# Linear attention: the column sums as dense passes in high and low part, and the values' planes in their result tile

## The chip, the cores and the metric

One core of a Trainium2 chip runs the whole layer. The metric is device microseconds of one execution, median over runs. TensorE (PE) multiplies, VectorE (DVE) and ScalarE (ACT) work elementwise, GpSimd (POOL) does a few elementwise steps, and nearly every transfer is issued from SyncE's queue (SP).

## The reference, cut to what matters

```python
u = rmsnorm(x, g_pre) @ W_in                     # q, k, v, gates of both head groups
log_a = log_sigmoid(g_lr @ w_a2 + b_a) / 16
# gated linear attention, 4 heads, dk = 128, dv = 256, with b = cumsum(log_a):
# scores[i, j] = sum_d q[i, d] k[j, d] exp(b[i, d] - b[j, d])   for j <= i
# out = scores @ v + (q exp(b)) @ state
# stick-breaking attention, 8 heads; then the output product, a norm,
# and a gated embedding product
```

1024 tokens, model width 2048, float32. The change touches only the scores of the linear attention, and the way its values get turned.

## The kernel before, in words

Every operand of a large product is split into a high part (`fp32r`, by a ScalarE copy) and a low part (what is left, by a VectorE subtraction); a product is the three matmuls high x high, low x high, high x low (`split`, L113; `dense`, L158). A "step" is one k-tile of a dense product for both halves of the tokens: six matmuls of 128x512.

The program writes the instructions of the small stages in between by generators. `dense` calls `step()` (L188) after each k-tile, and `step()` advances first the `urgent` generators (the turning of values) and then, at RATE_GLA = 1.0 step for step, the job in turn: `gla(h, ...)`, one linear-attention head at a time, while the projection of the next head's keys, queries and two value tiles runs on TensorE. The numbers W0, W1, W2 and W4 (L48) say how many steps the generator lets pass between its parts. The instructions of an engine are then put in order by a planner that goes by priority (the order of writing) and by what is ready; it can draw an instruction ahead whose inputs and buffer are there. Buffers are tagged (`BUFS`, L303): "E" and "X" have two, "u" twelve, "s" two, "o", "o2", "q" and "kt" one each.

A head is done in two halves of 512 tokens (four chunks of 128; of the second pair of chunks the order is reversed). Per half `gla` does:

1. The gate: one matmul, logarithms, cumulative sums b by four scans (L417 to L425). q exp(b) is made on GpSimd (L439), and the keys for the state in an "E" buffer (L437), which are then split in 16-bit planes by ScalarE and turned by a transposing transfer (`turn_by_dma`, L356).
2. The scores, chunk by chunk, by levels 64, 32, 16, 8, 4, 2, 1: for a level, `factors` (L443) makes k exp(..) and q exp(..) in an "X" buffer, `level` (L461) multiplies them by four matmuls of 128x128 into a "z" bank of PSUM, and `put` (L455) copies by a mask what belongs to the level into the scores `sc`. After level 8 the states are made.
3. Two parts of the scores are no matmul products but sums over the 128 partitions: the diagonal (sum of k*q, `prep_diag`, `put_diag`, L479 to L485) and level 1 (neighbours, `prep_one`, `put_one`, L488 to L500). They are made by `by_rows` (L468): ones with 32 columns against a float32 tile, in four tiles of the array, each giving 32 rows; then four masked copies of 32 partitions each. The diagonal's sums stand directly ahead of level 64, level 1's directly behind level 2.
4. The output of the half in "o" and "o2", its norm (whose mean is a column sum by two dense passes of ones against a high and a low part, `column_sums`, L198), and its store (L571).

Values get turned by `turn` (L364) after their projection: ScalarE splits the tile into planes of 16 bits in an "X" buffer, a transfer transposes them into an "E" buffer, and VectorE copies them together into the result tile (L369).

Of the kernel before, what the change touches and what calls it, by code (L numbers as in the profile page):

```python
# [12 lines left out]
F32R = mybir.dt.float32r  # L13
U8 = mybir.dt.uint8
U16 = mybir.dt.uint16
QT = 256
AF = mybir.ActivationFunctionType
ALU = mybir.AluOpType

P = 128  # L20
D = 2048
T = 1024
HT = 512
# [8 lines left out]
LEVELS = (64, 32, 16, 8, 4, 2, 1)  # L32
# [12 lines left out]


RATE_GLA = 1.0
W0, W1, W2, W4 = 2, 6, (2, 3, 3, 3, 2, 3), 2  # L48
RATE_SB = 0.9
W3 = 4  # L50
V_MID, V_END, VW = ("X", "X"), ("E", "E"), 3
L1, L2, PERIOD = 8, 8, 5
W = 2 * HT
KP = KT // 2
# [8 lines left out]
def layer(ctx, tc, xT, w_in, w_gate, w_lr, w_a2, b_a, g_pre, g_head, w_out, g_post,  # L63
          w_g, b_g, w_p, pT, ident, masks, sel_in, out):
    nc = tc.nc
    V, A, G, PE = nc.vector, nc.scalar, nc.gpsimd, nc.tensor
# [34 lines left out]
    def mm(o, lhsT, rhs, start, stop):  # L101
        PE.matmul(o, lhsT, rhs, start=start, stop=stop)  # L102

    def f(t):
        return t.bitcast(F32)
# [5 lines left out]
    ones_r = const.tile([P, P], F32R, name="ones_r")  # L111

    def split(hi, lo, src, eng=None):  # L113
        A.activation(hi, src, AF.Copy)  # L114
        (eng or V).tensor_tensor(lo, src, f(hi), op=ALU.subtract)  # L115
# [109 lines left out]
    pair = {}  # L225
# [76 lines left out]
    with tc.tile_pool(name="att", bufs=1, reuse_waits="tile") as ap:  # L302
# [11 lines left out]
        def at(tag, shape=(P, HT), dt=F32):  # L314
            pool, bufs = (ap, BUFS[tag]) if tag in BUFS else (own[1], {**GLA_BUFS, **SB_BUFS}[tag])
            return pool.tile(list(shape), dt, tag=tag, name=nm(tag), bufs=bufs)
# [37 lines left out]
            return go  # L354

        def turn_by_dma(src, n, mid, tag):  # L356
            pl = at(mid, (P, 2 * n), U16)
            A.activation(pl.rearrange("p (two n) -> p two n", two=2),  # L358
                         src.bitcast(U16)[:, :2 * n].rearrange("p (n two) -> p two n", two=2), AF.Copy)
            tt = at(tag, (P, 2 * n), U16)  # L360
            nc.sync.dma_start(tt.rearrange("p (c t) -> p c t", t=P), pl, transpose=True)
            return tt.rearrange("p (two c t) -> p two c t", two=2, t=P)

        def turn(vt, dst, parts):  # L364
            w = turn_by_dma(vt, HT, V_MID[parts - 1], V_END[parts - 1])
            for _ in range(VW):
                yield 1
            full = dst if parts == 1 else at("o")
            V.tensor_copy(full.bitcast(U16).rearrange("p (c t two) -> p two c t", c=4, two=2), w)  # L369
            if parts == 2:  # L370
                split(*dst, full)
            yield 1

        def view(t, start, *dims):
            return bass.AP(t.tensor, t.offset + start, [t.ap[0]] + [list(d) for d in dims])
# [28 lines left out]
        def gla(h, kp, qp, vp):  # L404
# [6 lines left out]
            for hf in HALVES:  # L411
# [25 lines left out]
                V.tensor_tensor(ke, ke, k, op=ALU.mult)  # L437
                turned_keys = turn_by_dma(ke, HT, "s", "E")
                G.tensor_tensor(qe, qe, q, op=ALU.mult)  # L439
                for _ in range(W0):  # L440
                    yield 1

                def factors(hl):  # L443
                    ref = view(b, hl - 1, (QT + 1, 2), (2 * hl, P // hl), (0, hl))
                    x = at("X")
                    xk = view(x, 0, (hl, 2), (2 * hl, P // hl), (1, hl))
                    xq = x[:, QT:].rearrange("p (s n h) -> p s n h", s=2, h=hl)
                    V.tensor_tensor(xk, ref, keys(b, hl), op=ALU.subtract)
                    V.tensor_tensor(xq, queries(b, hl), ref, op=ALU.subtract)
                    A.activation(x, x, AF.Exp, scale=1.0 / TAU)  # L450
                    times(xk, xk, keys(k, hl))
                    times(xq, xq, queries(q, hl))
                    return x

                def put(li, z):  # L455
                    hl = LEVELS[li]
                    m = mask_s[:, QT * li:QT * (li + 1)]
                    V.copy_predicated(queries(sc, hl), *(t.rearrange("p (s n h) -> p s n h", s=2, h=hl)
                                                         for t in (m, z[:, :QT])))
# [5 lines left out]
                        mm(to[:, :, j], ch(x, j), moving[:, :, j], True, True)  # L465
                    put(li, z)

                def by_rows(e, n, m):  # L468
                    z = ps("z")
                    rows = [slice(32 * g, 32 * g + 32) for g in range(4)]  # L470
                    for g, r in enumerate(rows):
                        PE.matmul(z[r, :4 * n].rearrange("p (c t) -> p c t", c=4), f(ones_r)[:, :32],
                                  view(e, n * g, (m, 4), (1, n)), start=True, stop=True,
                                  tile_position=(0, 32 * g))
                    return [(r, z[r, :4 * n]) for r in rows]

                def prep_diag():
                    e = at("E")
                    V.tensor_tensor(e, k, q, op=ALU.mult)  # L479
                    return e  # L480

                def put_diag(e):
                    for g, (r, z) in enumerate(by_rows(e, 32, P)):
                        m = mask_s[r, 7 * QT + 32 * g:7 * QT + 32 * g + 32].rearrange("p (c t) -> p c t", c=1)
                        V.copy_predicated(view(sc[r], 32 * g, (P, 4), (1, 32)), m.to_broadcast([32, 4, 32]),  # L485
                                          z.rearrange("p (c t) -> p c t", c=4))

                def prep_one():  # L488
                    e = at("E", (P, QT))
                    e4 = e.rearrange("p (s n h) -> p s n h", s=2, h=1)  # L490
                    V.tensor_tensor(e4, queries(b, 1), keys(b, 1), op=ALU.subtract)
                    A.activation(e, e, AF.Exp, scale=1.0 / TAU)
                    times(e4, e4, keys(k, 1))
                    times(e4, e4, queries(q, 1))
                    return e

                def put_one(e):
                    for g, (r, z) in enumerate(by_rows(e, 16, 64)):
                        with tc.high_priority(offset=800):
                            V.copy_predicated(view(sc[r], 32 * g + 1, (QT - 1, 2), (P, 2), (2, 16)),  # L500
                                              view(mask_s[r], 6 * QT + 16 * g, (P, 2), (64, 2), (1, 16)),
                                              z.rearrange("p (s c t) -> p s c t", s=2, c=2))

                def join_keys():
                    ket = at("kt")
# [14 lines left out]
                            V.scalar_tensor_tensor(S, Ss[-1], eb[:, c:c + 1], d, op0=ALU.mult, op1=ALU.add)  # L520
                        Ss.append(S)

                diag, xs = prep_diag(), factors(LEVELS[0])
                for _ in range(W1):
                    yield 1
                for i in range(6):
                    x, xs = xs, factors(LEVELS[i + 1]) if i < 5 else prep_one()
                    for _ in range(W2[i]):
                        yield 1
                    if i == 0:  # L530
                        ket = join_keys()
                        put_diag(diag)
                    level(i, x)
                    if i == 3:
                        states((0, 1))
# [918 lines left out]
```

## Time and profile before

| what | us |
|---|---|
| median of 3 runs | 2054.58 |
| lowest and highest | 2049.41, 2055.2 |
| profiled execution, its own time | 2058.89 |
| span of the profiled execution | 2057.2 |
| linear attention's stage | about 117 to 545 in the span |

The mean granted TensorE clock is 0.999 of full speed. In the tables of groups each row is a line of the kernel, an engine, an operation, its output and inputs by tile name, the shape and the count, then total busy us, mean ns of one, and the idle time of the engine ahead of it with what ended it. In a timeline each row has the start and the duration in us; a row with x4 stands for four instructions, and a note in brackets is idle time ahead of it with its releaser. Matmuls are pipelined, so the durations of neighbours overlap. L102 is the helper that issues all matmuls but the tiled ones (L472 here, L287 at the start); "dn" is a bank of a dense product, "z" a bank for the small stages.

### The profile page before, as it was taken

How to read it: one execution, taken by the hardware profiler on the slowest of the kernel's cores; microseconds unless marked ns; L12 is line 12 of the kernel's file. 1: busy time of each engine (PE TensorE's matmuls, PEld its weight loads, DVE VectorE, ACT ScalarE, POOL GpSimd, SP SyncE). 2: the span in 40 equal slices, each digit the busy share in tenths (PEclk: the TensorE clock that was granted, in tenths of full speed). 3: DMA queues.
4: the chain of work that ended last, by engine and by line, in shares of the span. 5: the costliest groups of instructions: out<-in, count | busy, mean ns of one | idle time of the engine just before them, and what ended most of it. 6: DMA issues, size and time to landing. Idle time of an engine off the chain costs nothing.

```text
span 2057.2 us, 26551 instructions
## 1 busy us (share of the span) xinstructions
PE 2041.2 (99%) x9632; PEld 1691.3 (82%) x9632; DVE 1466.2 (71%) x2305; ACT 865.9 (42%) x1367; POOL 92.5 (4%) x214
## 2 busy tenths in 40 slices
PE   9999999999999999999999999999999999999998
PEld 7788888888888788888888788888788888878887
DVE  8567777776666676666567677788778778886765
ACT  8333433333455455545457323344233434323332
POOL 0000000000101111101101000000000000000000
PEclk9999999999999999999999999999999999999999
DMA  7122333232244444434335798888888586876762
GB/s 236 53 79 83 89 82 94 82 88 82 86 105 108 96 111 109 115 93 93 79 98 158 262 330 287 310 292 300 315 289 282 167 307 224 301 272 218 235 202 92
DMA packets 237715, 354.90 MB, mean 173 GB/s; under 512 B 132736, under 2 KB 138000, under 8 KB 237584
## 3 DMA queue, kind: packets, MB, share of 16 engines
q1 hardware_dynamic: 236832, 350.97, 53.8%
q10 hardware_dynamic: 720, 2.23, 0.3%
q8 instruction: 75, 1.23, 0.3%
q14 instruction: 56, 0.46, 0.1%
q0 software_dynamic: 32, 0.01, 0.0%
HBM read 249.85 MB, written 73.92 MB: 157 GB/s over the span
## 4 chain that ended last, share of the span: by engine, by line
PE 77%; DVE 10%; DMA 8%; issue 3%; ACT 2%; POOL 0%; SPq 0%; DVEq 0%; POOLq 0%; ACTq 0%
PE dn L102 67%; PE z L102 4%; PE t L102 3%; PE o L102 2%; DVE wl L115 2%; DMA wr<-w_out 1%; DMA ar<-og_d 1%; DVE wr L936 1%; DMA E<-X 1%; DMA wr<-w_g 1%; DMA ar<-h_d 1%; DVE al L115 1%; DMA h_d<-st 1%; DVE ar L933 1%; DVE st L933 0%
## 5 line engine op out<-in xcount | busy, mean ns | idle before, releaser
L102 PE MATMUL dn<-ah,hi 128*128 128x512 f32 x1408 | 558.5, 397 | 1.0 <-ACT ah L271 1.0
L102 PE MATMUL dn<-ah,lo 128*128 128x512 f32 x1408 | 549.4, 390 | 0.0
L102 PE MATMUL dn<-al,hi 128*128 128x512 f32 x1408 | 548.8, 390 | 0.0
L102 PE MATMUL dn<-ah,wl 128*128 128x512 f32 x1216 | 474.4, 390 | 4.0 <-DVE wl L115 3.8
L102 PE MATMUL dn<-ah,wh 128*128 128x512 f32 x1216 | 473.4, 389 | 1.0 <-ACT wh L114 1.0
L102 PE MATMUL dn<-al,wh 128*128 128x512 f32 x1216 | 473.1, 389 | 0.0
L102 PEld LDWEIGHTS dn<-al,hi 128*128 128x128 f32 x1408 | 264.3, 188 | 56.7 <-DVE al L272 0.3
L102 PEld LDWEIGHTS dn<-ah,hi 128*128 128x128 f32 x1408 | 265.0, 188 | 55.0 <-ACT ah L271 3.1
L102 PEld LDWEIGHTS dn<-ah,lo 128*128 128x128 f32 x1408 | 265.1, 188 | 48.5
L114 ACT ACTIVATE wh<-wr 128x1024 fp32r<-128x1024 f32 x152 | 159.7, 1057 | 295.9 <-PE dn L102 221.2
L102 PEld LDWEIGHTS dn<-ah,wl 128*128 128x128 f32 x1216 | 228.3, 188 | 55.1 <-DVE wl L115 7.8
L102 PEld LDWEIGHTS dn<-ah,wh 128*128 128x128 f32 x1216 | 228.3, 188 | 48.8 <-ACT wh L114 2.0
L102 PEld LDWEIGHTS dn<-al,wh 128*128 128x128 f32 x1216 | 228.3, 188 | 47.3
L115 DVE TENSOR_TENSOR wl<-wr,wh 128x1024 fp32r<-128x1024 f32 x152 | 185.1, 1219 | 10.5 <-ACT wh L114 10.3
L114 ACT ACTIVATE hi<-raw 128x512 fp32r<-128x512 f32 x192 | 120.1, 626 | 149.4 <-PE dn L102 146.1
L115 DVE TENSOR_TENSOR lo<-raw,hi 128x512 fp32r<-128x512 f32 x192 | 131.4, 685 | 53.4 <-ACT hi L114 53.1
L358 ACT ACTIVATE X<-E 128x256 uint16<-128x256 uint16 (+2 forms) x96 | 81.1, 844 | 130.7 <-DVE E L640 65.5
L635 DVE TENSOR_TENSOR_SCAN X<-X 128x128 f32<-128x128 f32 (+2 forms) x96 | 98.0, 1021 | 15.7 <-POOL X L629 14.2
L650 DVE COPY v<-E 128x512 uint16<-128x512 uint16 (+1 forms) x160 | 64.3, 429 | 47.3 <-DMA E<-X 44.1
L115 DVE TENSOR_TENSOR s<-v,s 128x512 fp32r<-128x512 f32 (+1 forms) x82 | 52.6, 642 | 61.5 <-ACT s L114 58.2
L936 DVE TENSOR_TENSOR wr<-wr,wr 128x1024 f32<-128x1024 f32 x48 | 58.7, 1222 | 43.7 <-DMA wr<-w_out 21.8
L933 DVE TENSOR_TENSOR wr<-wr,wr 128x1024 f32<-128x1024 f32 x48 | 58.7, 1224 | 41.2 <-DMA wr<-w_g 30.6
(246 smaller groups left out, 2205.8 us busy)
## 6 DMA issues: line engine op xcount, KB each, us to landing
raw<-w_in SPq DMA_DIRECT2D x160, 256.0 KB, 2.6
wr<-w_g SPq DMA_DIRECT2D x64, 512.0 KB, 4.3
wr<-w_out SPq DMA_DIRECT2D x56, 512.0 KB, 4.5
wr<-w_gate SPq DMA_DIRECT2D x40, 512.0 KB, 4.8
g_d<-wr SPq DMA_DIRECT2D x32, 512.0 KB, 3.7
wr<-g_d SPq DMA_DIRECT2D x32, 512.0 KB, 4.9
ar<-h_d SPq DMA_DIRECT2D x28, 512.0 KB, 5.0
ar<-og_d SPq DMA_DIRECT2D x25, 512.0 KB, 5.5
```

The source lines that it names most:

```text
L102: PE.matmul(o, lhsT, rhs, start=start, stop=stop)
L114: A.activation(hi, src, AF.Copy)
L115: (eng or V).tensor_tensor(lo, src, f(hi), op=ALU.subtract)
L358: A.activation(pl.rearrange("p (two n) -> p two n", two=2), src.bitcast(U16)[:, :2 * n].rearrange("p (n two) -> p two n", two=2), AF.Copy)
L635: V.tensor_tensor_scan(rev, rev, rev, initial=kq[:, n:n + 1], op0=ALU.mult, op1=ALU.bypass)
L650: V.tensor_copy(to[:, :, :m, j], w[:, :, 2 * g:2 * g + m])
L933: V.tensor_tensor(dst, a, b, op=ALU.add)
L936: V.tensor_tensor(dst, a, b, op=ALU.subtract)
```

## The change

- The tiled column sums (`by_rows`) are gone. Both sums are made by `add_up`: ones with 128 columns against a high part and a low part, two dense passes into one bank. For the diagonal they have 512 columns, for level 1 256.
- The parts come from `split`: for the diagonal the product k*q now goes into "o", its high part into "o2" and its low part into "kt" (three tiles that are idle then), and all of that is written ahead of the W0 pause. For level 1 the high part goes into an "X" buffer and the low part into an "E" buffer.
- Each of the two is put into the scores by one masked copy on 128 partitions instead of four on 32.
- The diagonal's sums are made W5 = 7 steps after the W0 pause, which is two steps ahead of level 64 and one step earlier than before; levels 64, 32 and 16 come one step later than before, the others as before (W1 and W2 are changed to that).
- The planes of the linear attention's values are written into the result tile itself ("u") and no longer into an "X" buffer; the transfer reads them there, and the copy then overwrites them.

```diff
--- before.py
+++ after.py
@@ -45,10 +45,11 @@
 
 
 RATE_GLA = 1.0
-W0, W1, W2, W4 = 2, 6, (2, 3, 3, 3, 2, 3), 2
+W5 = 7
+W0, W1, W2, W4 = 2, 7, (2, 3, 3, 2, 2, 3), 2
 RATE_SB = 0.9
 W3 = 4
-V_MID, V_END, VW = ("X", "X"), ("E", "E"), 3
+VW = 3
 L1, L2, PERIOD = 8, 8, 5
 W = 2 * HT
 KP = KT // 2
@@ -354,7 +355,7 @@
             return go
 
         def turn_by_dma(src, n, mid, tag):
-            pl = at(mid, (P, 2 * n), U16)
+            pl = at(mid, (P, 2 * n), U16) if isinstance(mid, str) else mid.bitcast(U16)
             A.activation(pl.rearrange("p (two n) -> p two n", two=2),
                          src.bitcast(U16)[:, :2 * n].rearrange("p (n two) -> p two n", two=2), AF.Copy)
             tt = at(tag, (P, 2 * n), U16)
@@ -362,7 +363,7 @@
             return tt.rearrange("p (two c t) -> p two c t", two=2, t=P)
 
         def turn(vt, dst, parts):
-            w = turn_by_dma(vt, HT, V_MID[parts - 1], V_END[parts - 1])
+            w = turn_by_dma(vt, HT, dst if parts == 1 else "X", "E")
             for _ in range(VW):
                 yield 1
             full = dst if parts == 1 else at("o")
@@ -437,6 +438,9 @@
                 V.tensor_tensor(ke, ke, k, op=ALU.mult)
                 turned_keys = turn_by_dma(ke, HT, "s", "E")
                 G.tensor_tensor(qe, qe, q, op=ALU.mult)
+                diag, pair = at("o"), (at("o2", dt=F32R), at("kt", dt=F32R))
+                V.tensor_tensor(diag, k, q, op=ALU.mult)
+                split(*pair, diag)
                 for _ in range(W0):
                     yield 1
 
@@ -465,25 +469,18 @@
                         mm(to[:, :, j], ch(x, j), moving[:, :, j], True, True)
                     put(li, z)
 
-                def by_rows(e, n, m):
+                def add_up(hi, lo):
+                    n = hi.shape[-1]
                     z = ps("z")
-                    rows = [slice(32 * g, 32 * g + 32) for g in range(4)]
-                    for g, r in enumerate(rows):
-                        PE.matmul(z[r, :4 * n].rearrange("p (c t) -> p c t", c=4), f(ones_r)[:, :32],
-                                  view(e, n * g, (m, 4), (1, n)), start=True, stop=True,
-                                  tile_position=(0, 32 * g))
-                    return [(r, z[r, :4 * n]) for r in rows]
-
-                def prep_diag():
-                    e = at("E")
-                    V.tensor_tensor(e, k, q, op=ALU.mult)
-                    return e
-
-                def put_diag(e):
-                    for g, (r, z) in enumerate(by_rows(e, 32, P)):
-                        m = mask_s[r, 7 * QT + 32 * g:7 * QT + 32 * g + 32].rearrange("p (c t) -> p c t", c=1)
-                        V.copy_predicated(view(sc[r], 32 * g, (P, 4), (1, 32)), m.to_broadcast([32, 4, 32]),
-                                          z.rearrange("p (c t) -> p c t", c=4))
+                    mm(z[:, :n], ones_r, hi, True, False)
+                    mm(z[:, :n], ones_r, lo, False, True)
+                    return z
+
+                def put_diag(x):
+                    c4 = "p (c t) -> p c t"
+                    V.copy_predicated(sc.rearrange(c4, c=4),
+                                      mask_s[:, 7 * QT:7 * QT + P].rearrange(c4, c=1).to_broadcast([P, 4, P]),
+                                      add_up(*x).rearrange(c4, c=4))
 
                 def prep_one():
                     e = at("E", (P, QT))
@@ -492,14 +489,13 @@
                     A.activation(e, e, AF.Exp, scale=1.0 / TAU)
                     times(e4, e4, keys(k, 1))
                     times(e4, e4, queries(q, 1))
-                    return e
-
-                def put_one(e):
-                    for g, (r, z) in enumerate(by_rows(e, 16, 64)):
-                        with tc.high_priority(offset=800):
-                            V.copy_predicated(view(sc[r], 32 * g + 1, (QT - 1, 2), (P, 2), (2, 16)),
-                                              view(mask_s[r], 6 * QT + 16 * g, (P, 2), (64, 2), (1, 16)),
-                                              z.rearrange("p (s c t) -> p s c t", s=2, c=2))
+                    hi, lo = at("X", (P, QT), F32R), at("E", (P, QT), F32R)
+                    split(hi, lo, e)
+                    return hi, lo
+
+                def put_one(x):
+                    with tc.high_priority(offset=800):
+                        put(6, add_up(*x))
 
                 def join_keys():
                     ket = at("kt")
@@ -520,8 +516,11 @@
                             V.scalar_tensor_tensor(S, Ss[-1], eb[:, c:c + 1], d, op0=ALU.mult, op1=ALU.add)
                         Ss.append(S)
 
-                diag, xs = prep_diag(), factors(LEVELS[0])
-                for _ in range(W1):
+                xs = factors(LEVELS[0])
+                for _ in range(W5):
+                    yield 1
+                put_diag(pair)
+                for _ in range(W1 - W5):
                     yield 1
                 for i in range(6):
                     x, xs = xs, factors(LEVELS[i + 1]) if i < 5 else prep_one()
@@ -529,7 +528,6 @@
                         yield 1
                     if i == 0:
                         ket = join_keys()
-                        put_diag(diag)
                     level(i, x)
                     if i == 3:
                         states((0, 1))
```

## The prediction

> **What bounds the kernel now.** First the page's head, for the share of the engines.
>
> ```profile
> span 2057.2 us, 26551 instructions
> PE 2041.2 (99%) x9632; PEld 1691.3 (82%) x9632; DVE 1466.2 (71%) x2305; ACT 865.9 (42%) x1367; POOL 92.5 (4%) x214
> ```
>
> TensorE is busy for 2041.2 of 2057.2 us: what the change does to the time is what it does to the matmul stream and to the few waits in it. VectorE at 71% and ScalarE at 42% have room on average, so work added to them costs only where a matmul then waits.
>
> Second, the list of waits of TensorE, cut to the stage of the linear attention (100 to 545 us). It has three rows (total us, times, longest):
>
> ```profile
> PE z L472 <- DVE E L479: 1.0, 4, 0.3
> PE z L102 <- DVE E L115: 0.2, 1, 0.2
> PE z L102 <- DVE X L153: 0.2, 1, 0.2
> ```
>
> L472 are the tiled column sums that the change takes out, L479 is the product k*q for the diagonal. So four of the eight halves (four heads, two halves of 512 tokens) wait there; the other two rows, the heads' norm and a level's factors, come to 0.4 us.
>
> Third, the timeline of TensorE, because a duration is no price here. A dense matmul of 512 columns lasts 0.39 us, but the next one starts sooner:
>
> ```profile
> 302.02 0.39 PE L102 MATMUL dn<-ah,lo 128*128 128x512 f32 x1
> ...
> 303.61 0.39 PE L102 MATMUL dn<-al,hi 128*128 128x512 f32 x1
> ```
>
> Seven steps lie between these starts: 1.59/7 = 0.227 us each. That is the price of a 512-column matmul in a full stream, and I price each inserted block by how far it pushes the dense stream back: time from the last dense start ahead of it to the second dense start behind it (the first one behind a block is held up too), less two steps (0.454).
>
> **What the old sums cost.** The diagonal's sums and level 64 are one block, in a half that doesn't wait and in one that does; then a level alone:
>
> ```profile
> 130.91 0.39 PE L102 MATMUL dn<-al,hi 128*128 128x512 f32 x1
> 131.23 0.42 PE L472 MATMUL z<-E,ones_r 128*32 128x128 f32 x8
> 131.59 0.71 PE L102 MATMUL z<-X 128*128 128x128 f32 x4
> 132.06 0.48 PE L102 MATMUL dn<-ah,hi 128*128 128x512 f32 x1
> 132.37 0.39 PE L102 MATMUL dn<-ah,lo 128*128 128x512 f32 x1
> ```
>
> ```profile
> 182.69 0.39 PE L102 MATMUL dn<-al,hi 128*128 128x512 f32 x1
> 183.33 0.43 PE L472 MATMUL z<-E,ones_r 128*32 128x128 f32 x8 [0.25 <-DVE E L479]
> ...
> 184.47 0.39 PE L102 MATMUL dn<-ah,lo 128*128 128x512 f32 x1
> ```
>
> ```profile
> 136.03 0.39 PE L102 MATMUL dn<-al,hi 128*128 128x512 f32 x1
> ...
> 136.93 0.40 PE L102 MATMUL dn<-ah,lo 128*128 128x512 f32 x1
> ```
>
> The last fence holds one level's four matmuls and the first dense one behind them in its gap. Level alone: 136.93 - 136.03 - 0.454 = 0.45 us. Diagonal with level 64: 132.37 - 130.91 - 0.454 = 1.01 us, so the diagonal costs 0.56 us; in the half that waits 184.47 - 182.69 - 0.454 = 1.33 us, so 0.88 us. The 0.32 between the two is the wait. Part of the 0.56 is the entry: 0.32 us from the last dense start to the first tile, where 0.227 is usual. Eight records stand there for four matmuls of the program, since each float32 one runs as two.
>
> Level 1 comes behind level 2 in one block:
>
> ```profile
> 153.72 0.39 PE L102 MATMUL dn<-al,hi 128*128 128x512 f32 x1
> ...
> 154.49 0.32 PE L472 MATMUL z<-E,ones_r 128*32 128x64 f32 x8
> 154.73 0.50 PE L102 MATMUL dn<-ah,hi 128*128 128x512 f32 x1
> 155.07 0.40 PE L102 MATMUL dn<-ah,lo 128*128 128x512 f32 x1
> ```
>
> 155.07 - 153.72 - 0.454 = 0.90 us, less the level: level 1 costs 0.45 us.
>
> **What the new sums cost.** The very form, ones against a high and a low part with 512 columns, is in the trace: the sums of the heads' norm. For 256 columns the nearest rows are three matmuls of the stick-breaking scores.
>
> ```profile
> 220.35 0.39 PE L102 MATMUL dn<-al,hi 128*128 128x512 f32 x1
> 220.58 0.39 PE L102 MATMUL z<-X,ones_r 128*128 128x512 f32 x1
> 220.81 0.39 PE L102 MATMUL z<-E,ones_r 128*128 128x512 f32 x1
> 221.03 0.39 PE L102 MATMUL dn<-ah,hi 128*128 128x512 f32 x1
> ```
>
> ```profile
> 545.29 0.39 PE L102 MATMUL dn<-al,hi 128*128 128x512 f32 x1
> 545.52 0.28 PE L102 MATMUL z<-b,st 128*128 128x256 f32 x1
> 545.63 0.28 PE L102 MATMUL z<-u,st 128*128 128x256 f32 x1
> 545.75 0.28 PE L102 MATMUL z<-b,st 128*128 128x256 f32 x1
> ...
> 546.11 0.40 PE L102 MATMUL dn<-ah,lo 128*128 128x512 f32 x1
> ```
>
> The pair of 512 columns pushes the stream back by 221.03 - 220.35 - 0.227 = 0.45 us, with no entry and no exit to pay. The three of 256 take 546.11 - 545.29 - 0.454 = 0.37 us, 0.12 each, so a pair 0.24. Behind level 1's tiles the first dense matmul is held up by 155.07 - 154.73 - 0.227 = 0.11 us; if a pair of 256 spares the block this exit, it comes to 0.13 or so. I keep 0.24.
>
> Per half the diagonal gives back 0.56 - 0.45 = 0.11 us, or 0.88 - 0.45 = 0.43 where the wait goes too, and level 1 gives back 0.45 - 0.24 = 0.21. Over the kernel: 4 x 0.11 + 4 x 0.43 + 8 x 0.21 = 0.44 + 1.72 + 1.68 = 3.8 us with the wait gone, 2.5 us with a wait of the same size left.
>
> Here the Trainium skill speaks against the change. Its page "TensorEngine Tiling (Array Packing)", section Theoretical Speedup, gives up to four times the speed where one dimension is 32 or less, since tiles load and multiply at the same time (Key Properties); by that the eight 128-column records should take no longer than two of them. The trace doesn't agree: 131.59 - 131.23 = 0.36 us pass until the level's matmul starts, not 2 x 128/512 x 0.227 = 0.11. By the rule the sums would come to rival (b). The same section says that a change of the tiling mode drains the array; the late entry (0.32 against 0.227) agrees.
>
> **The other engines.** The groups of VectorE and ScalarE, in total busy us and mean ns, the linear attention's stage:
>
> ```profile
> L115 DVE TENSOR_TENSOR lo<-raw,hi 128x512 fp32r<-128x512 f32 x70 | 47.8, 683 | 6.4 <-ACT hi L114 6.4
> L458 DVE COPY_PREDICATED s<-mask,z 128x256 f32<-128x256 uint8 x48 | 23.3, 485 | 19.1 <-PE z L102 18.7
> L500 DVE COPY_PREDICATED s<-mask,z 32x64 f32<-32x64 uint8 x32 | 9.5, 296 | 1.1
> L485 DVE COPY_PREDICATED s<-mask,z 32x128 f32<-32x128 uint8 x32 | 9.5, 296 | 0.3
> L114 ACT ACTIVATE hi<-raw 128x512 fp32r<-128x512 f32 x70 | 43.9, 627 | 94.3 <-PE dn L102 94.3
> ```
>
> Diagonal on VectorE: out go four copies of 0.296 (1.18 us); in come a subtraction of 0.68 and one copy of 128x512, which no row has: between 0.485 (L458, half as long) and twice that, 0.97; I take 0.9, since the columns grow and not the partitions. Net +0.4 us a half. Level 1: out four copies (1.18), in one copy of 0.485 and a subtraction of 256 columns, at most 0.68 and about 0.4: net -0.3. ScalarE gets at most 0.63 + 0.63. So VectorE's total stays, and ScalarE's 42% covers its share. No DMA is added. The planes of the values move from the X buffers into the result tile that is allotted anyway: no instruction more, one X buffer freed sooner. The copy that fills this tile already waits for the transpose that now also reads it. Its price is the tile being written earlier; I put it at nothing, because the transfers around it are waited for by VectorE and not by a matmul. If that cover fails, the planes' ScalarE instruction waits, and behind it on ScalarE the high parts of the weights.
>
> **The wait that could come.** The diagonal's chain gets longer: product, high part on ScalarE, low part on VectorE, sums. And the sums come a step earlier: after 2 + 7 = 9 steps where it was 2 + 6 + 2 = 10, a step being six matmuls, 1.36 us. In the half above TensorE reaches them at 183.33 - 0.32 - 1.36 = 181.65 us. VectorE, ScalarE and SyncE there:
>
> ```profile
> 178.88 0.42 DVE L448 TENSOR_TENSOR X<-b 128x256 f32<-128x256 f32 x1
> ...
> 181.69 1.58 DVE L479 TENSOR_TENSOR E<-u,u 128x512 f32<-128x512 f32 x1
> ```
>
> ```profile
> 180.60 1.06 ACT L358 ACTIVATE s<-E 128x1024 uint16<-128x1024 uint16 x1 [0.30 <-DVE E L437]
> ```
>
> ```profile
> 175.79 0.98 SPq L571 DMA_DIRECT2D o_d<-o  x2
> ```
>
> ```profile
> DMA to landing us min/median/max: 2.0/2.0/3.2
> ```
>
> The product started at 181.69, the moment ScalarE had read the key product out of the E buffer (180.60 + 1.06 = 181.66): it waited for one of the two E buffers, while L448 of level 64, written behind it in the program, ran 2.8 us ahead of it. In the change it stands in o, whose last user, the store of the half before (L571), has landed by 175.79 + 2.0 to 178.0 or so. VectorE's order follows what is ready (L448 shows it), so I expect the product at about 178.9, where L448 stood: 178.9 + 0.7, high part 0.63, low part 0.68, some handing over: ready at about 181.1, half a microsecond ahead of 181.65. Behind it on VectorE queue level 64's factors, needed two steps (2.7 us) after the sums, so a shift of 0.7 is covered. The cover is thin: L479 took 1.58 us where its twin subtraction takes 0.68, and if such a 0.9 us falls into the chain, it ends at 182.0 and the wait is 0.35, as large as now. Bounds: wait gone (-3.8) or kept (-2.5). I take the middle, -3.2 us.
>
> The profiled execution took 2058.89 us for a span of 2057.2, 4.3 us over the median; -3.2 there makes 2055.7, and on the median of 2054.58 it makes **2051.4**.
>
> **The rivals.** (a) Slower: the product is not moved up, and follows L479's old place. It ends at 183.27, high and low part add 1.31, 184.6: a wait of 2.9 us in each of four halves, 11.7 us. Without it the edit gives 2.5, so +9.2 us: 2063.8. For it: VectorE stands full around this place, and the chain has two engines more. Against it: what held L479 was the E buffer, and o is free. It decides from a wait of about 1 us in each of the four halves on. (b) The old sums were cheaper than their blocks: the tiles ran beside each other, and entry and exit belong to the levels. Two records of 128 columns by the dense rate are 0.11 us, of 64 columns 0.06, so each half would lose 0.34 + 0.18, 4.2 us in all: 2058.8. The rows speak against it: 0.36 us from the first tile of the diagonal to the level's matmul (131.23 to 131.59), 0.24 from that of level 1 to the dense one (154.49 to 154.73). By the rule of the Trainium skill's tiling page it would come out as in (b). (c) More than the sums: the freed X and E buffers also take away the two other waits of this stage (0.4 us in the list; L472's 0.25 there pushes the stream by 0.32, so about 0.5), and level 2's exit is spared (8 x 0.11 = 0.9): -3.8 - 0.5 - 0.9 = -5.2 us, 2049.4. (d) Nothing happens: the sums are equal in cost and the wait stays, 2054.6.
>
> **How the numbers follow.** What a measurement of this kernel can tell from no change is about 0.3%, 6.2 us: the three runs shown lie 5.8 us apart. My forecast (-2.5 to -3.8) gets 0.52, (c) 0.26, (d) 0.07, (b) 0.05, (a) 0.10. With the scatter of the runs (about 3 us each way on a median) (c) goes past 0.3% in half its cases, the forecast in one of seven: 0.13 + 0.07 makes faster 0.20, (a) makes slower 0.09, the rest, 0.71, stays within. The range reaches from (c) less the scatter, 2045, to (b) and half of (a), 2059.
>
> **What would show it.** In the profile after: no tiled records; blocks of two 512-column matmuls on ones alone in the dense stream, pushing it by 0.45 us; level 64 alone, 0.45; level 2 with a pair of 256, about 0.69 where it was 0.90. The list of waits names the low part (L115) ahead of the diagonal's sums, with under 0.4 us in at most four halves. The product stands ahead of the levels' factors. Rival (a) would show waits of over 1 us there; (b) a block of the sums longer than 0.5 us. What would prove me wrong is a sum of the blocks that falls by 3 us while the span does not: a wait elsewhere, in the values' turn for instance.

## The result, and the profile after

The changed kernel takes 2051.26 us, the kernel before 2055.53 us (medians of 22 runs each); the ratio is 0.9977, 95% interval 0.9972 to 0.9983. By the ratio that is 4.7 us less (3.5 to 5.8), by the two medians 4.3 us. The forecast was 2051.4 us, 3.2 us less.

The head of the page of after, beside that of before:

```profile
span 2051.0 us, 26377 instructions
PE 2037.4 (99%) x9536; PEld 1694.8 (83%) x9536; DVE 1460.0 (71%) x2273; ACT 872.2 (43%) x1383; POOL 94.7 (5%) x214
```

Of TensorE's instructions 96 are gone: 128 tiled records out, 32 dense passes in. VectorE's busy time is 6 us less and ScalarE's 6 us more. The two profiles differ by 6.2 us, more than the medians, so the part that belongs to the change has to be cut out. A stage can be timed by two landmarks of the timeline of TensorE, the first gate matmul and the first stick-breaking score. In before:

```profile
117.31 0.39 PE L102 MATMUL z<-lr,a2c 128*128 128x512 f32 x1
...
543.82 0.22 PE L102 MATMUL z<-b,st 128*128 128x128 f32 x1
```

In after:

```profile
116.25 0.39 PE L103 MATMUL z<-lr,a2c 128*128 128x512 f32 x1
...
538.24 0.22 PE L103 MATMUL z<-b,st 128*128 128x128 f32 x1
```

The stage went from 426.5 to 422.0 us: 4.5 us, between what the medians and the ratio say. The other 1.7 us lie ahead of the stage and behind it, where the change did nothing (over the twelve experiments the first landmark lies anywhere from 116.0 to 117.3). All experiments are read by this stage as well as by their ratio.

The waits of TensorE within the stage, after:

```profile
PE z L103 <- DVE X L154: 0.7, 1, 0.7
```

The four waits ahead of the diagonal's sums are gone, and so are the two others; one new wait has come. Now the new blocks, timeline of TensorE of after: the diagonal's sums, then level 2 with level 1.

```profile
179.75 0.39 PE L103 MATMUL dn<-al,hi 128*128 128x512 f32 x1
179.98 0.39 PE L103 MATMUL z<-o,ones_r 128*128 128x512 f32 x1
180.21 0.39 PE L103 MATMUL z<-kt,ones_r 128*128 128x512 f32 x1
180.44 0.39 PE L103 MATMUL dn<-ah,hi 128*128 128x512 f32 x1
```

```profile
152.54 0.39 PE L103 MATMUL dn<-al,hi 128*128 128x512 f32 x1
152.77 0.38 PE L103 MATMUL z<-X 128*128 128x128 f32 x2
152.91 0.36 PE L103 MATMUL z<-X,ones_r 128*128 128x256 f32 x1
153.11 0.28 PE L103 MATMUL z<-E,ones_r 128*128 128x256 f32 x1
153.23 0.38 PE L103 MATMUL z<-X 128*128 128x128 f32 x2
...
153.68 0.39 PE L103 MATMUL dn<-ah,lo 128*128 128x512 f32 x1
```

The first block pushes the dense stream back by 180.44 - 179.75 - 0.227 = 0.46 us, and by 0.45 to 0.46 in each of the eight halves, with no wait. The second pushes by 153.68 - 152.54 - 0.454 = 0.69 us counted to the second dense start, and by 0.72 counted to the last dense start ahead of the next block; before, the block was 0.90 and 0.96 in the same two ways.

Counted to that last dense start throughout, the stage's 4.5 us come out as five terms:

- The diagonal with level 64: 9.5 us before (four halves at 1.03, four at 1.35) and 7.3 after, -2.2.
- Level 1: 8 x (0.96 - 0.72), -1.9.
- The two other waits: -0.9 (the list puts them at 0.4, but the stream is pushed back by 0.5 and 0.4).
- The new wait: +1.0.
- The output blocks behind level 1 in the first halves, which pushed by 2.38 us in three and 2.33 in the fourth, and push by 2.24 now: -0.5.

The last term belongs to level 1's tiles too. Wherever level 1 is in tiles once (the kernel before, experiments 1, 3, 4 and 10), the output block in three of the first halves is at 2.37 to 2.38 us; wherever level 1 is dense (experiment 2 among them, where nothing else is changed), it is at 2.24 to 2.25. Behind the tiles the dense starts stay 0.236 us apart for a while instead of 0.227 (155.07, 155.31, 155.55, 155.78 in before); why is not shown.

Last, the diagonal's chain that the forecast followed, VectorE and ScalarE of after:

```profile
177.23 0.17 DVE L434 COPY eb<-q 128x4 f32<-128x4 f32 x1
177.30 0.69 DVE L442 TENSOR_TENSOR o<-u,u 128x512 f32<-128x512 f32 x1
...
178.84 0.69 DVE L116 TENSOR_TENSOR kt<-o,o 128x512 fp32r<-128x512 f32 x1
```

```profile
178.02 0.63 ACT L115 ACTIVATE o<-o 128x512 fp32r<-128x512 f32 x1
```

The product stands directly behind the small copy `eb`, ahead of all factors. The low part ends at 179.53, the sums start at 179.98.

### The profile page after: what moved, and what is told of

The parts are those of the page before. It is cut to its first block, busy times and chain, and to the rows that moved or that the text cites. A ratio compares the mean times of both kernels' runs of the same rounds, so it can differ in the third digit from the quotient of the medians.

```text
span 2051.0 us, 26377 instructions
## 1 busy us (share of the span) xinstructions
PE 2037.4 (99%) x9536; PEld 1694.8 (83%) x9536; DVE 1460.0 (71%) x2273; ACT 872.2 (43%) x1383; POOL 94.7 (5%) x214
## 4 chain that ended last, share of the span: by engine, by line
PE 77%; DMA 9%; DVE 8%; issue 3%; ACT 2%; SPq 0%; POOL 0%; DVEq 0%; ACTq 0%; POOLq 0%
PE dn L103 68%; PE z L103 4%; PE t L103 3%; PE o L103 2%; DMA E<-X 2%; DMA wr<-w_out 2%; DVE wl L116 2%; DMA wr<-w_g 1%; DVE wr L934 1%; DMA ar<-og_d 1%; DMA ar<-h_d 1%; DVE al L116 1%; DMA h_d<-st 1%; DVE X L633 1%; DVE ar L934 1%
```

## The experiments

Each kernel was timed in five rounds beside the kernel before on the same chip. "Stage" is the time between the two landmarks in its profile; it is that of one execution, and lies up to some 2 us from what the ratio says.

| kernel | ratio to before, 95% interval | stage, us | against before |
|---|---|---|---|
| before | 1 | 426.5 | |
| the change | 0.9977 (0.9972 to 0.9983) | 422.0 | -4.5 |
| diagonal dense alone | 1.0015 (1.0007 to 1.0024) | 429.8 | +3.3 |
| level 1 dense alone | 1.0008 (0.9998 to 1.0017) | 425.4 | -1.1 |
| planes alone | 0.9999 (0.9989 to 1.0009) | 426.4 | -0.1 |
| product early, tiles kept | 0.9989 (0.9979 to 0.9998) | 425.6 | -0.9 |
| before, tiles twice | 1.0008 (0.9998 to 1.0018) | 429.8 | +3.3 |
| change, dense passes twice | 1.0007 (0.9999 to 1.0016) | 427.6 | +1.1 |
| change, product in E | 1.0044 (1.0028 to 1.0060) | 435.2 | +8.7 |
| change, sums behind the levels | 0.9985 (0.9977 to 0.9994) | 422.1 | -4.4 |
| change, planes back in X | 1.0011 (0.9999 to 1.0022) | 431.1 | +4.6 |
| change, level 1 back in tiles | 0.9998 (0.9988 to 1.0007) | 426.3 | -0.2 |
| change, old steps | 0.9980 (0.9971 to 0.9989) | 422.3 | -4.2 |
| change, levels in pairs | 1.0003 (0.9995 to 1.0012) | 427.7 | +1.2 |

My theory at first: each part is worth what its blocks push the matmul stream back, and the parts add up. The rivals are named in the expectations.

**1. The diagonal's sums alone.**

```diff
 # the kernel before, with the change's add_up, put_diag, early product and split, W5, W1 and W2
+                put_diag(pair)                       # 7 steps after W0, two passes of 512 columns
-                        put_diag(diag)               # tiles ahead of level 64
```

> Only the diagonal's sums are changed (dense passes of 512 columns, product in o, parts in o2 and kt, two steps ahead of level 64, the pauses W as in the change); level 1 keeps its tiles, the values' planes stay in X. Theory (each block costs what it pushes the matmul stream back): 4 x 0.11 + 4 x 0.43, so about -2.2 us; in the profile a block of two passes alone, 0.45 us, no wait ahead of it. Rival (b) (tiles cheap): 8 x 0.34, +2.7 us less the wait of 1.3, so +1.4 us. Rival (wait and buffers only): the whole -4.7 us of the change comes from the wait and the freed X and E buffers, then this one has only the wait, -1.3 us.

Slower: 1.0015. The blocks came as expected (0.45 us, but for one half with a wait of 0.3 for the low part), and yet the stage is 3.3 us longer. The waits of TensorE in its stage:

```profile
PE z L103 <- DVE X L154: 3.8, 5, 1.1
PE o L103 <- DVE s L506: 0.5, 1, 0.5
PE z L103 <- DVE kt L116: 0.3, 1, 0.3
```

Five times a level waits for its factors in X. No theory of mine had this: the gain of the blocks was there and was spent on another wait.

**2. Level 1's sums alone.**

```diff
 # the kernel before
-                    return e                          # prep_one; by_rows in put_one
+                    hi, lo = at("X", (P, QT), F32R), at("E", (P, QT), F32R)
+                    split(hi, lo, e)
+                    return hi, lo
```

> Only level 1's sums are changed (split and two dense passes of 256 columns); the diagonal keeps its tiles, the planes stay in X. Theory: 8 x 0.2 to 0.24, so -1.6 to -1.9 us; the block of level 2 with level 1 pushes by about 0.7 us where it was 0.95. Rival (b): 8 x 0.18, +1.4 us. Rival (wait and buffers only): 0.

1.0008, with an interval that just takes in no change; the stage is 1.1 us shorter. Again the block itself is as expected (0.7 us), and again there are new waits:

```profile
PE z L102 <- DVE s L492: 1.1, 1, 1.1
PE z L472 <- DVE E L486: 1.0, 4, 0.3
PE z L102 <- DVE X L153: 0.6, 1, 0.6
```

The middle row is the old wait for the product; the first and the last (a level's bank not yet copied out, factors late) are new or grown.

**3. The planes alone.**

```diff
-            pl = at(mid, (P, 2 * n), U16)
+            pl = at(mid, (P, 2 * n), U16) if isinstance(mid, str) else mid.bitcast(U16)
-            w = turn_by_dma(vt, HT, V_MID[parts - 1], V_END[parts - 1])
+            w = turn_by_dma(vt, HT, dst if parts == 1 else "X", "E")
```

> Only the values' planes are moved into their result tile; both sums keep their tiles. Theory: no matmul is added or taken out, so 0, at best -0.5 us from the waits of factors in X; the four waits ahead of the diagonal's tiles stay (0.3 us each). Rival (wait and buffers only): the freed X buffer takes the waits away, -1.3 to -2.2 us.

No change: 0.9999, stage -0.1 us. The four waits for the product stay, and the one row for factors in X is gone from the list. Taken alone the planes are worth nothing, as the prediction had it.

**4. The product early, tiles kept.**

```diff
+                diag = at("o")                        # ahead of the W0 pause
+                V.tensor_tensor(diag, k, q, op=ALU.mult)
-                    e = at("E")                       # prep_diag
-                    V.tensor_tensor(e, k, q, op=ALU.mult)
```

> The product k*q goes into o and is written ahead of the W0 pause, as in the change, but is not split: the tiled sums stay where they were, and so does everything else. Theory: the product no longer waits for an E buffer, the four waits ahead of the tiles go (4 x 0.32), -1.3 us, and the entry into the tiles stays (0.32 us from the last dense start to the first tile where 0.227 is usual). Rival (the wait was for something else, the values or GpSimd): waits stay, 0.

0.9989, stage -0.9 us: the four waits are gone from the list, which holds one row only, a new wait of 0.6 us for factors. So an early place in a buffer of its own is enough; which of the two it takes is tried in experiment 7. The late entry into the tiles stays:

```profile
182.03 0.39 PE L102 MATMUL dn<-al,hi 128*128 128x512 f32 x1
182.35 0.43 PE L474 MATMUL z<-o,ones_r 128*32 128x128 f32 x8
```

0.32 us from the last dense start to the first tile, now with the product long there.

**5. The tiles twice.**

```diff
 # the kernel before, by_rows
-                    for g, r in enumerate(rows):
+                    for g, r in list(enumerate(rows)) * 2:
```

> The kernel before with every tiled sum made twice into the same bank (the second writes the same numbers): 64 more matmuls of the program, 128 more records, nothing else. Theory: the second set pushes the stream by what the first takes between its first tile and what follows, 0.36 us for the diagonal and 0.24 for level 1: 8 x 0.60, +4.8 us. Rival (b) (tiles run beside each other, and the cost lay in entry and exit): 8 x (0.11 + 0.06), +1.4 us.

Neither. The stage is 3.3 us longer, of which some 1 us are three waits for factors, larger or new; the blocks show the price of the second set without them (diagonal, then level 1):

```profile
129.76 0.39 PE L102 MATMUL dn<-al,hi 128*128 128x512 f32 x1
130.08 0.64 PE L472 MATMUL z<-E,ones_r 128*32 128x128 f32 x16
...
131.43 0.39 PE L102 MATMUL dn<-ah,lo 128*128 128x512 f32 x1
```

```profile
152.79 0.39 PE L102 MATMUL dn<-al,hi 128*128 128x512 f32 x1
...
153.55 0.43 PE L472 MATMUL z<-E,ones_r 128*32 128x64 f32 x16
...
154.25 0.39 PE L102 MATMUL dn<-ah,lo 128*128 128x512 f32 x1
```

131.43 - 129.76 - 0.454 = 1.22 where one set had 1.01: 0.21 us. 154.25 - 152.79 - 0.454 = 1.01 where one set had 0.90: 0.11 us. So eight records cost 0.21 and 0.11 us once the array is in tiles, where eight dense records of 128 and of 64 columns would by the rate of 0.227 for 512 columns come to 0.45 and 0.23: twice as fast by that rate. (Dense records of 128 columns don't reach that rate here. They push by 0.11 us each, experiment 12, and against that the tiles are four times as fast.) But the first set costs 0.56 and 0.45: some 0.35 us at each of the sixteen places do not depend on how much is done in tiles.

That this is the price of getting into the tiles and out again is the likeliest reading. Its nearest rival is the type, since the tiled sums are float32 in a stream of fp32r. The levels speak against it: a level's product is float32 as well, two matmuls of the program that show as four records (not four matmuls, as the description of the kernel before has it), and eight such records push by 0.90 where four push by 0.45 (experiment 12), which leaves nothing for a change of type. The Trainium skill, on its page "TensorEngine Tiling (Array Packing)" (section Key Properties), says that different tiles work at the same time and that a change of the tiling mode drains the array. The trace agrees with the first and shows 0.35 us that fit the second, the larger of the two here; that it is a drain no run shows.

**6. The dense passes twice.**

```diff
 # the changed kernel, add_up
+                    for _ in range(2):
                         mm(z[:, :n], ones_r, hi, True, False)
                         mm(z[:, :n], ones_r, lo, False, True)
```

> The changed kernel with both passes of every column sum made twice into the same bank: 32 more matmuls. Theory: 0.45 us more for the diagonal and 0.24 to 0.26 for level 1 in each half: 8 x 0.70, +5.6 us over the changed kernel, so about +1 us against the kernel before. Rival (b): the dense passes cost the same here; it differs in the tiles alone.

As expected: 1.0007 against before, and the stage is 5.6 us longer than the changed kernel's (427.6 to 422.0). Dense passes are priced by the stream alone; nothing hides them.

**7. The product in an E buffer.**

```diff
-                diag, pair = at("o"), (at("o2", dt=F32R), at("kt", dt=F32R))
+                diag, pair = at("E"), (at("o2", dt=F32R), at("kt", dt=F32R))
```

> The changed kernel with the product k*q in an E buffer in place of o, so that it again has to wait until the keys' planes are read. Theory: the product comes at its old time, low part some 1.5 us later; where the planner knows it the sums move a step later in the stream, and what it doesn't know is a wait: 0 to 4 x 1 us, so +0 to +4 us over the changed kernel, with the row L116 or L115 named ahead of the diagonal's sums. Rival (the place of the product doesn't matter): equal to the changed kernel, no wait.

Far more than expected: 1.0044 against before, the stage 13.2 us longer than the changed kernel's. The waits:

```profile
PE z L103 <- ACT o L115: 7.3, 7, 1.7
PE z L103 <- DVE kt L116: 2.9, 3, 1.0
PE z L103 <- DVE X L154: 0.4, 1, 0.4
```

And the product in the half that was followed in the prediction (VectorE, this kernel):

```profile
181.10 1.58 DVE L442 TENSOR_TENSOR E<-u,u 128x512 f32<-128x512 f32 x1
```

It is back at its old place, with its old 1.58 us: written as early as in the change, but held by the E buffer. This is the prediction's rival (a), made real: in the four second halves TensorE waits 1.6 to 1.7 us, and in three of the first halves 1.2 to 1.4 us in two pieces (high part, then low part). Counted by the push, the four cost 7.7 us and the three 5.6.

**8. The sums behind their levels.**

```diff
-                put_diag(pair)                        # 7 steps after W0
+                        level(i, x)                   # i == 0
+                        put_diag(pair)
-                        put(6, add_up(*x))            # drawn ahead, between level 2's pairs
+                    z = add_up(*x)                    # behind level 2
```

> The changed kernel with the diagonal's passes directly behind level 64's four matmuls, and level 1's passes behind all of level 2's (they stood between its two pairs): each block then ends in a pass of 512 or 256 columns and not in one of 128. Theory: the first dense matmul behind such a block is no longer held up, 0.1 us a block, 16 blocks: -1.6 us at most, -0.8 if level 1's passes of 256 don't cover it; blocks of about 0.82 and 0.65 us. Rival (the hold-up belongs to any block of small matmuls): equal to the changed kernel.

The rival holds. The block of level 64 with the diagonal:

```profile
132.06 0.39 PE L103 MATMUL dn<-al,hi 128*128 128x512 f32 x1
132.28 0.60 PE L103 MATMUL z<-X 128*128 128x128 f32 x4
132.65 0.48 PE L103 MATMUL z<-o,ones_r 128*128 128x512 f32 x1
132.96 0.40 PE L103 MATMUL z<-kt,ones_r 128*128 128x512 f32 x1
133.19 0.39 PE L103 MATMUL dn<-ah,hi 128*128 128x512 f32 x1
```

Now the first pass on ones is the one held up (132.65 to 132.96, 0.31 us where 0.227 is usual), and the block pushes by 0.91 us, just what the two apart did. Level 2 with level 1 pushes by 0.70 us, where it was 0.72. The stage is as long as the changed kernel's, but its waits are others: level 64 is late in three of the first halves (+0.4 us each), and the last half's wait ahead of level 8 (1.0) is gone.

**9. The planes back in X.**

```diff
 # the changed kernel
-            w = turn_by_dma(vt, HT, dst if parts == 1 else "X", "E")
+            w = turn_by_dma(vt, HT, "X", "E")
```

> The changed kernel with the values' planes back in an X buffer, nothing else undone. Theory now (the planes, the high part of level 1 and the levels' factors share two X buffers): factors come late and the matmuls of single levels wait for them, 0.4 to 1.4 us each, five or more in the stage, so +3 to +6 us over the changed kernel; the two runs that had dense sums and planes in X showed such waits. Rival (the prediction's price): planes at nothing, equal to the changed kernel.

1.0011 against before where the change has 0.9977: 0.34%, 7 us lost by undoing this one step. Waits of TensorE in its stage, and the row of VectorE's waits that matters:

```profile
PE z L103 <- DVE X L154: 6.0, 5, 3.0
```

```profile
DVE X L452 <- DMA E<-X: 13.8, 8, 3.9
```

VectorE's first step of a level's factors (L452) waits eight times for the transpose that reads the planes out of the X buffer; in after this row has 2.2 us in two. From there it goes on to the matmul of the level.

The stage of this profile shows 9.1 us and not 7, and some 2.9 of them are no wait. Behind the longest one the dense starts are 0.43 us apart instead of 0.227, at a granted TensorE clock of 0.50 (timeline, then busy time of the engines from 412 to 418 us with the clock after POOL's column):

```profile
412.74 1.20 PE L103 MATMUL z<-X 128*128 128x128 f32 x4 [2.96 <-DVE X L154]
...
416.29 0.63 PE L103 MATMUL dn<-al,hi 128*128 128x512 f32 x1
416.72 0.63 PE L103 MATMUL dn<-ah,hi 128*128 128x512 f32 x1
```

```profile
412.00:418.00 6.00, 5.26 (x19) 4.71 (x19) 4.80 (x13) 1.26 (x2) 0.00 (x0) 0.50 0.27 87
```

None of the shorter waits in the stage of before, after or experiment 7 is followed by such a stretch.

**10. Level 1 back in tiles.**

```diff
-                    hi, lo = at("X", (P, QT), F32R), at("E", (P, QT), F32R)
-                    split(hi, lo, e)
-                    return hi, lo
+                    return e                          # prep_one; put_one by by_rows, as before
```

> The changed kernel with level 1 back in tiles: dense sums for the diagonal and the planes in their result tile. Theory: the diagonal's part is worth its blocks once X is free: from the first gate matmul to the first stick-breaking score the stage is some 2.2 us shorter than before, against 4.5 us for the whole change, and has no wait for factors. Rival (the two sums depend on each other): stage as long as before or longer.

0.9998, stage -0.2 us: the rival is nearer. The diagonal's blocks are at 0.45 us in seven halves, but the last half waits 0.9 us for factors, one half 0.3 us for the low part, and an output matmul 0.6 us for the scores. So level 1's dense form is worth 4.3 us on top of this kernel: 1.9 in its own blocks, 0.5 in the output blocks behind them, and most of the rest in these waits.

This kernel and that of experiment 1 differ in the planes alone. They are 3.5 us apart, by the stage and by the ratio. So the same move of the planes is worth nothing in the kernel before, 3.5 us with the diagonal dense, and 7 us with both sums dense.

**11. The old steps for levels 32, 16 and 8.**

```diff
-W0, W1, W2, W4 = 2, 7, (2, 3, 3, 2, 2, 3), 2
+W0, W1, W2, W4 = 2, 7, (2, 2, 3, 3, 2, 3), 2
```

> The changed kernel with levels 32, 16 and 8 at the steps that they had before (pauses 2, 2, 3, 3, 2, 3): only level 64 stays a step later. Theory: the one wait left in the changed kernel, 0.87 us ahead of level 8 in the last half, goes, -0.9 us. Rival (levels 32 and 16 are then short of time): new waits for X ahead of them, +0.3 us or more in each of several halves.

Equal to the change (0.9980, stage 422.3). The wait of the last half is not gone; it has moved from level 8 to level 32:

```profile
503.19 0.57 PE L103 MATMUL z<-X 128*128 128x128 f32 x3 [0.95 <-DVE X L154]
```

What makes it is seen in the changed kernel (ScalarE, then VectorE): in the last half the values being turned are those of the first stick-breaking head, whose planes the change leaves in X.

```profile
505.00 1.04 ACT L359 ACTIVATE X<-v 128x1024 uint16<-128x1024 uint16 x1
```

```profile
509.25 0.43 DVE L452 TENSOR_TENSOR X<-b 128x256 f32<-128x256 f32 x1 [1.16 <-DMA E<-X]
```

**12. Levels in pairs.**

```diff
-W0, W1, W2, W4 = 2, 7, (2, 3, 3, 2, 2, 3), 2
+W0, W1, W2, W4 = 2, 7, (2, 0, 5, 0, 5, 3), 2
```

> The changed kernel with levels taken in pairs (pauses 2, 0, 5, 0, 5, 3): 64 with 32, 16 with 8, then 4, then 2. Theory from the run with the sums behind their levels (whatever follows a block of 128-column matmuls is held up by 0.1 us, a dense pass too): each pair pays it once, 2 x 8 x 0.1, -1.6 us at most, blocks of about 0.82 us for two levels. Rival (both X buffers are then held until the pair is through, and the next factors come late): waits ahead of level 16 or 4 that eat it, 0 or slower.

Slower than the change, 1.0003 against before, by waits for factors (5.1 us in seven, ahead of level 32). And the pair saves nothing even where it doesn't wait:

```profile
132.38 0.39 PE L103 MATMUL dn<-al,hi 128*128 128x512 f32 x1
132.61 1.05 PE L103 MATMUL z<-X 128*128 128x128 f32 x8
...
133.73 0.40 PE L103 MATMUL dn<-ah,lo 128*128 128x512 f32 x1
```

133.73 - 132.38 - 0.454 = 0.90 us for eight records, twice the 0.45 of four. There is no exit to spare: every record of 128 columns pushes the stream by 0.11 us, and the late start behind the block is only where the last one's share shows.

No version beat the change beyond its interval.

## Why the prediction was right, and where it was not

The time was hit to 0.14 us, and that is chance. The forecast took 3.2 us off a median of three runs (2054.58) that lies 1.0 below the median of 22. The saving itself was forecast too small: 3.2 us where 3.5 to 5.8 were measured, and by size rival (c) with 5.2 is nearer. What decides between the two are the parts.

- **What the new sums cost:** right. The pair of 512 columns was priced at 0.45 us and pushes by 0.45 to 0.46; the pair of 256 at 0.24, and it is 0.72 - 0.46 = 0.26. Experiment 6 confirms both by the time.
- **What the old sums cost:** right for the diagonal (0.56 or 0.88), 2.2 us saved where 2.16 stood in the working. Level 1 was put at 0.45; counted to the end of the dense run it is 0.50, and 0.5 us in all lie in the output blocks behind it, which the prediction left out. What stood behind these sizes was wrong in part: I read the 0.36 us from the tiles to the level's matmul as the array being held by the tiles. Experiment 5 shows 0.21 for the tiles themselves (0.11 for level 1), and the rest as a price that does not grow with them. Rival (b) had the tiles nearer and the total wrong, since that price left with the tiles.
- **The wait:** right. The product moved to the place that was named, and the chain ended 0.45 us ahead of the sums where half a microsecond was said. The product took 0.69 us there and not 1.58. The term that was mis-sized is the half of the wait that I kept for safety (0.6 us): none came. Experiments 4 and 7 show the cause to be the E buffer.
- **The values' planes, priced at nothing:** this step failed. Alone they are worth nothing (experiment 3), but in the changed kernel they carry 7 us (experiment 9). The reason given was that the transfers around X are waited for by VectorE and not by a matmul. That holds in the kernel before but for one wait of 0.2 us, since its levels have slack. With a split more on VectorE, level 1's high part in X and level 8 one step closer to level 16, VectorE's wait for X reaches the matmul (experiments 1 and 9; experiment 2 has one such wait of 0.6 us, but experiment 4 has it too, without a split). Level 1's high part is not needed for all of it, since experiments 1 and 10 show 3.5 us with level 1 in tiles; beyond that, which of the three takes the slack was not separated.
- **The sum:** right, since the prediction summed all parts of one kernel and the planes' cover was there. As a sum of parts it would have failed: alone they give +3.3, -1.1 and -0.1 us in the stage, together -4.5. The other waits that went (0.9) were in rival (c), at 0.5, and the new one (1.0) in none; that they cancel is luck. That leaves the kept half of the wait (0.6), level 1's blocks (1.9 for 1.7) and the output blocks (0.5) between the 3.2 forecast and the 4.5 measured.
- **Rival (a):** did not happen; experiment 7 makes it happen and finds +13.2 us over the change in the stage, where it was priced at 11.7 for four halves. Each of those waits 1.6 to 1.7 us, not 2.9, but three of the first halves wait too.
- **Rival (c)'s spared exit:** does not exist (experiments 8 and 12).

## What to carry to other kernels

Price an insertion into a full matmul stream by how far it pushes the next dense starts, not by durations: that gave the blocks here to a few hundredths of a microsecond. A small tiled product in the middle of a dense stream pays a fixed price, here 0.35 us against 0.1 to 0.2 for its own work, so a dense pass with four times the columns can be the cheaper one. And an edit that frees a buffer can measure as nothing by itself and still carry the whole gain of the edits beside it: undo the parts from the finished kernel, besides trying each alone.

## What the runs showed of the hardware that was not expected

- Tiles of 32 columns: 0.21 us for eight records of 128 columns, 0.11 for eight of 64, and beside that a fixed 0.35 us or so for each excursion into tiles.
- A record of 128 columns with weights of its own pushes the stream by 0.11 us and one of 256 columns by 0.12 to 0.13, where 512 columns take 0.227: going from 256 columns to 128 saves next to nothing here.
- The masked copy on VectorE from PSUM takes 0.296 us for 32 x 64 and for 32 x 128, and 0.724 us for 128 x 512 in the changed kernel: four small copies cost more than the large one. Of the 128 x 256 copies into the scores those of levels 64 to 4 take 0.42 to 0.46 us, those of levels 2 and 1 about 0.73, though they are as large; their columns lie in runs of two and of one.
- After one wait of TensorE of 3.0 us the granted clock was 0.50 for 6.8 us (experiment 9), and the stretch cost 2.9 us on top of the wait.
